# An encoder layer on one core: how far ahead expert outputs come back from DRAM, and the order of work where two stages meet

## The chip, the cores and the metric

The kernel runs on one NeuronCore of a Trainium2 chip. The metric is the device time of one execution in microseconds, lower is better. The core has five engines, each with its own in-order instruction queue: PE (matrix products), DVE (VectorE), ACT (ScalarE), POOL (GpSimd) and SP (SyncE). In this kernel SP issues nearly all plain transfers and POOL the indirect ones, which gather rows by index. All transfers are carried by 16 DMA engines. An instruction waits in its queue on semaphores, and everything behind it on that queue waits too.

## The reference, cut to what matters

One layer for 512 tokens of width 1024 in float32: layer norm, two kinds of attention, a projection and a second norm, then the part that this change is about, a mixture of 16384 single-neuron experts, and a gate and a last norm.

```python
q  = (xb @ w_q).reshape(PEER_CHUNK, PEER_HEADS, PEER_KEY_DIM)   # 8 heads
s1 = einsum('thd,kd->thk', q[..., :half], sub_keys[0])          # 128 keys
s2 = einsum('thd,kd->thk', q[..., half:], sub_keys[1])
# best 16 of each, best 16 of their sums: expert number e1 * 128 + e2
g   = softmax(cv)                        # 8 * 16 = 128 picks a token
u   = u_table[idx]                       # rows of a 16384 x 1024 table
act = g * gelu(einsum('td,ted->te', xb, u))
ffn = einsum('te,ted->td', act, v_table[idx])
h   = layer_norm(alpha * h + ffn + sigmoid(h @ W_g + b_g) * (p @ W_ple))
```

Each token picks 128 of 16384 experts. U and V, the two tables, have 64 MiB each.

## The kernel before, in words

The 512 tokens lie in four chunks of 128. They go three ways.

- **Chunk 0 by gathered rows.** For each of its 128 picks POOL fetches 128 rows of U (512 KB, tile `gat`, `GATS` = 8 buffers), and DVE multiplies them with the tokens and sums (`gather_u`, L1281). After a GELU the same is done with V rows, added into `base` (`gather_v`, L1290 and L1292). These 257 steps are spread over other work.
- **Chunks 1 to 3 densely.** The experts are 128 blocks of 128. A matrix G of gate weights (tokens by experts) is built and written to DRAM (`g_dram`). In the last long stage, the V stage, G of eight blocks is loaded at a time (`gt`, 1.5 MB, two buffers). For each block it is split into a high and a low part, V's block (512 KB, `v_raw` or `raw`) is split the same way, and PE does 18 products into six accumulators (`expert_out`).
- Dense tokens also need GELU of tokens times U. For **chunk 1** this comes from gathered U rows while routing goes on (`own_rows`), and is folded into G. For **chunks 2 and 3** (256 tokens) PE multiplies with each block of U: tile `ge`, 128 KB a block, multiplied into `gt` at L1379.

The `ge` of the first `LEAD` = 107 blocks are made early, as plain float32 products (`lead_block`, L1088), while DVE and POOL route tokens, build G and gather. Those of the first `SPILL` = 96 blocks are written to DRAM (`ge_dram`, L1072), the others are kept in SBUF. The remaining blocks get theirs inside the V stage (`expert_in`), with a split of U by ACT and DVE and 24 products.

The V stage takes the blocks in the order 96 to 127, then 0 to 95. So it first uses the kept outputs and those made along the way, and from its 33rd block on those that come back from DRAM. Block n of the stage reloads the `ge` of block n + `GE_AHEAD` (L1374, on SP). All `ge` tiles, at first writing, in `expert_in` and at reload, rotate over `GES` = 13 buffers in the order in which they are made, and a new one waits until the tile `GES` before it has been read.

What sets the order around the change: DVE and SP follow the order in which the V stage's code is written, and at the seam before it all five engines do. In block n the code asks for the G load (when due), the V load, the reload, the multiply L1379, the splits, the products, and then some gathered rows. V loads of the late blocks alternate between two sets of three buffers, `v_raw` for even n and `raw` for odd n. Until block 128 - `LEAD` the rows advance by a full share a block, later by half a share (`LATE`); all shares together are 128 - 0.5 `LEAD` - 4, which is 70.5.

The **seam** is the block of code between routing and the V stage. `BESIDE` rows of chunk 0 have been gathered before it, up to `PRE` by its end. `blocks_ahead` advances the lead blocks on PE, `cut_v` splits V's first two blocks, and `load_g` brings the first eight blocks of G on POOL's queue in two parts, of which the second part holds the tokens whose G is written last.

Of the kernel before, what the change touches and what calls it, by code (L numbers as in the profile page):

```python
# [32 lines left out]
N_U = N_D - N_S  # L33
GT = 32
GB = 8
LEAD = 107
SPILL = 96
FIRST = 8
PACE = 1.1
AHEAD = 14.0  # L40
LAG = 6.0
PRE = 42
BESIDE = 24
OWN = 1.2
OWN_G = 0.65
OWN_LATE = 10.0
# [6 lines left out]
NA_FROM = (0, 64, 192, 256)  # L53
GATS = 8
NO_GATHER = 1
GE_AHEAD = 12
GES = 13
RAWS = 4
LOW = -3.0e38
FEED_NA = 2.85  # L60
# [8 lines left out]
def tile_encoder_layer(ctx: ExitStack, tc: tile.TileContext, A: dict, out: bass.AP):  # L69
# [651 lines left out]
    for kk in range(4):  # L721
        w = stream(A["w_o"][kk * 256:(kk + 1) * 256, 0:512].rearrange("(k p) n -> p k n", p=128), [2, 512])
        for k2 in range(2):
            k = 2 * kk + k2
# [330 lines left out]
    def load_u():  # L1055
        nonlocal loaded
        if loaded < LEAD:
            if loaded % RAWS == RAWS - 1 and loaded < LEAD - 16:
                raw = rg.tile([128, 8, 128], F32, name="raw_u")
# [18 lines left out]
    def lead_block():  # L1078


        while len(raws) < (RAWS if loaded < LEAD - 16 else 3) and loaded < LEAD:
            load_u()
# [171 lines left out]
    def in_wst(n):  # L1254

        return n % 2 and 128 - LEAD < n < 124

    def load_v(n):
        raw = wst.tile([128, D], F32, name="raw", bufs=3) if in_wst(n) else pV.tile([128, D], F32, name="v_raw", bufs=3)
        nc.sync.dma_start(raw, v_rows[order[n] * 128:(order[n] + 1) * 128, :])  # L1260
        return raw
# [11 lines left out]
    def fetch_u(c, k):  # L1273
        u = pG.tile([128, D], F32, name="gat", bufs=GATS)
        nc.gpsimd.indirect_dma_start(out=u[:], out_offset=None, in_=u_rows,  # L1275
                                     in_offset=bass.IndirectOffsetOnAxis(ap=i_sel[:, c, k:k + 1], axis=0))
        return u

    def gather_u(c, k, u=None):
        u = fetch_u(c, k) if u is None else u  # L1280
        nc.vector.scalar_tensor_tensor(scr, u, 1.0, h[c], op0=OP.mult, op1=OP.mult,  # L1281
                                       accum_out=hdot[:, c, k:k + 1])
# [32 lines left out]
    def blocks_ahead(n):  # L1315
        for _ in range(8 * n):
            next(pe_work, None)
# [4 lines left out]
    with tc.manual_schedule(engines={nc.vector.engine, nc.scalar.engine, nc.tensor.engine, nc.sync.engine,  # L1322
                                     nc.gpsimd.engine}):
        gating = True
        some = [fetch_u(0, BESIDE + k) for k in range(4)]
        gt_next = load_g(0, nc.gpsimd, ((128 // GT, NTG), (0, 128 // GT)))
        some += [fetch_u(0, BESIDE + k) for k in range(4, GATS - 1)]
        blocks_ahead(2)
        v_next = [load_v(n) for n in range(2)]
        for u in range(4):  # L1330
            gather_u(0, BESIDE + u, some[u])
        blocks_ahead(2)
        v_next.append(load_v(2))
        v_cut = {}
        for n in range(2):
            v_cut[n] = cut_v(n)
            blocks_ahead(1)
        for u in range(4, 7):
            gather_u(0, BESIDE + u, some[u])
        blocks_ahead(2)  # L1340
        for k in range(BESIDE + 7, PRE):
            gather_u(0, k)
        for _ in pe_work:
            pass
    done, spent = PRE, 0
    with tc.manual_schedule(engines={nc.vector.engine, nc.sync.engine}):
        expert_in(LEAD)
        for n, i in enumerate(order):
            if n % GB == 0:
                gt = gt_next  # L1350
            if n % GB == (GB // 2 if n < 128 - LEAD + 4 else GB - 2) and n // GB < 128 // GB - 1:
                gt_next = load_g(n // GB * GB + GB)
# [37 lines left out]
            if n >= NO_GATHER:  # L1390
                spent += 1 if n + LEAD < 128 else LATE
            upto = min(len(steps), PRE + math.ceil((len(steps) - PRE) * spent / (128 - (1 - LATE) * LEAD - 3 - NO_GATHER)))
            for f in steps[done:upto]:
# [107 lines left out]
```

## Time and profile before

| | |
|---|---|
| median of 3 runs | 1694.06 us (1692.46 to 1695.3) |
| the profiled execution's own time | 1681.8 us |
| its span, first to last instruction | 1679.9 us |
| mean granted clock of PE | 0.97 |
| busy share: PE, DVE, ACT, POOL | 92%, 77%, 39%, 33% |
| moved by DMA | 462.00 MB, 275 GB/s over the span |

By stage (the view of busy time in stretches; share is the mean busy share of the 16 DMA engines, which can come out slightly above 1):

| stretch, us | what | PE busy, us | DVE busy, us | clock | DMA share | GB/s |
|---|---|---|---|---|---|---|
| 0 to 470 | norms, attention, queries | 456.35 | 344.01 | 1.00 | 0.37 | 115 |
| 470 to 893 | routing, building G, lead blocks, chunk 1's rows | 409.61 | 378.56 | 1.00 | 0.99 | 381 |
| 893 to 950 | the seam | 49.54 | 25.53 | 0.94 | 0.93 | 359 |
| 950 to 1090 | V stage, blocks with `expert_in` | 139.22 | 129.94 | 0.99 | 1.03 | 403 |
| 1090 to 1625 | V stage, blocks without | 449.83 | 379.13 | 0.93 | 0.86 | 307 |
| 1625 to 1680 | last blocks, last norm | 45.20 | 44.58 | 0.93 | 0.30 | 112 |

How to read the lines shown below. In the page's digits a span is cut into 40 slices of 42 us, a digit is the busy share in tenths. In a list by time the columns are start, duration, engine, line, operation, tiles, and in brackets the idle time before and what ended it. PE's durations overlap when products follow each other, so starts tell its pace. In a list of waits, who waited is left of the arrow, and behind the colon stand the total in us, how often, and the longest. A stretch has its bounds, length, then busy us with the count of instructions for PE, PEld (weight loads), DVE, ACT and POOL, then clock, DMA share and GB/s. A DMA queue's row has packets, MB and its share of the 16 engines' time: q1 is SP's queue, q0 POOL's.

### The profile page before, as it was taken

What the parts mean: (1) busy time and instruction counts of PE and PEld (TensorE: products, weight loads), DVE (VectorE), ACT (ScalarE), POOL (GpSimd) and SP (SyncE); (2) the same over time, 40 slices, a digit from 0 to 9 for tenths busy, and PEclk for the clock granted to TensorE, in tenths of its full rate; (3) what the DMA queues carried; (4) which work ended last, traced back from release to release, by engine and by line L of the source; (5) the groups of instructions that cost most, each with busy time, mean ns of one, the idle gap of its engine ahead of it and who ended that gap; (6) DMA issues with size and microseconds to landing.
All of it is one profiled execution on the core that took longest, in us unless ns stands there. A gap on an engine that the chain in (4) does not pass through costs nothing.

```text
span 1679.9 us, 22935 instructions
## 1 busy us (share of the span) xinstructions
PE 1549.7 (92%) x7691; PEld 1278.8 (76%) x7691; DVE 1301.7 (77%) x3019; ACT 659.5 (39%) x1235; POOL 552.8 (33%) x522
## 2 busy tenths in 40 slices
PE   8999899999999999999898899978888878888787
PEld 5788677888888888888797788866666666666666
DVE  6466784799899988988894699977677766777677
ACT  3356683433226642762353243322222222222233
POOL 1013100100143335333342555543345444445420
PEclk9999999999999999999999999999899988999999
DMA  6342330432699999999898999988788888888881
GB/s 218 84 126 75 96 107 1 141 89 65 219 340 341 401 400 410 396 415 415 287 387 340 405 406 402 399 296 306 277 310 316 314 295 292 302 312 325 295 321 76
DMA packets 195178, 462.00 MB, mean 275 GB/s; under 512 B 17778, under 2 KB 98546, under 8 KB 193524
## 3 DMA queue, kind: packets, MB, share of 16 engines
q1 hardware_dynamic: 121104, 214.07, 35.9%
q0 software_dynamic: 58400, 208.69, 33.4%
q10 hardware_dynamic: 15556, 37.76, 5.9%
q8 instruction: 61, 1.00, 0.2%
q14 instruction: 57, 0.47, 0.1%
HBM read 415.64 MB, written 41.94 MB: 272 GB/s over the span
## 4 chain that ended last, share of the span: by engine, by line
PE 38%; DMA 27%; DVE 19%; issue 10%; ACT 4%; POOL 1%; SPq 1%; ACTq 0%; DVEq 0%; POOLq 0%
DMA v_raw<-in_v_rows_dram 15%; PE mm L1088 4%; PE hp L1088 4%; PE mm L107 3%; PE tr L980 3%; PE mm L109 3%; PE pj L107 3%; PE mm L108 3%; PE pj L108 3%; DVE base L1292 3%; PE pj L109 3%; DMA raw<-in_uT_dram 3%; DMA whi<-in_u_rows_dram,s_ix 2%; DVE scr L1281 2%; DVE wlo L93 2%
## 5 line engine op out<-in xcount | busy, mean ns | idle before, releaser
L1290 POOL DMA_INDIRECT gat<-in_v_rows_dram,i_sel x128 | 208.5, 1629 | 250.1 <-DVE base L1292 213.9
L107 PE MATMUL acc<-v_hi,a_hi 128*128 128x512 f32 x450 | 185.2, 417 | 61.2 <-ACT v_hi L92 49.8
L92 ACT CAST whi<-raw 128x1024 fp32r<-128x1024 f32 (+4 forms) x117 | 117.3, 1003 | 199.3 <-DMA raw<-in_v_rows_dram 82.5
L1088 PE MATMUL mm<-whole,raw 128*128 128x256 f32 x848 | 192.0, 380 | 1.2 <-DMA raw<-in_uT_dram 1.2
L108 PE MATMUL acc<-v_lo,a_hi 128*128 128x512 f32 x450 | 183.2, 410 | 4.7 <-DVE v_lo L93 4.6
L109 PE MATMUL acc<-v_hi,a_lo 128*128 128x512 f32 x450 | 183.9, 412 | 0.0
L93 DVE TENSOR_TENSOR v_lo<-v_raw,v_hi 128x1024 fp32r<-128x1024 f32 x75 | 91.9, 1225 | 108.4 <-ACT v_hi L92 106.0
L1088 PEld LDWEIGHTS mm<-whole,raw 128*128 128x128 f32 x848 | 159.0, 191 | 21.9 <-DMA raw<-in_uT_dram 1.6
L1275 POOL DMA_INDIRECT gat<-in_u_rows_dram,i_sel x104 | 133.3, 1282 | 120.9 <-DVE scr L1281 99.2
L93 DVE TENSOR_TENSOR wlo<-raw,whi 128x1024 fp32r<-128x1024 f32 (+4 forms) x117 | 135.6, 1160 | 38.4 <-ACT whi L92 37.2
L1292 DVE SCALAR_TENSOR_TENSOR base<-gat,hdot,base 128x1024 f32<-128x1024 f32 x128 | 164.0, 1282 | 1.6
L107 PEld LDWEIGHTS acc<-v_hi,a_hi 128*128 128x128 f32 x450 | 89.0, 199 | 88.6 <-ACT v_hi L92 55.0
L92 ACT CAST v_hi<-v_raw 128x1024 fp32r<-128x1024 f32 x75 | 78.8, 1050 | 174.2 <-DMA v_raw<-in_v_rows_dram 167.5
L107 PE MATMUL acc<-whi,a_hi 128*128 128x512 f32 x306 | 123.5, 405 | 19.3 <-ACT a_hi L92 19.3
L92 ACT CAST a_hi<-gt 128x384 fp32r<-128x384 f32 x126 | 64.6, 512 | 191.8 <-DVE gt L1379 182.5
L1281 DVE SCALAR_TENSOR_TENSOR scr<-gat,h 128x1024 f32<-128x1024 f32 x104 | 127.2, 1223 | 10.7 <-DMA gat<-in_u_rows_dram,i_sel 8.7
L93 DVE TENSOR_TENSOR a_lo<-gt,a_hi 128x384 fp32r<-128x384 f32 x126 | 69.8, 554 | 72.1 <-ACT a_hi L92 72.1
L109 PE MATMUL acc<-whi,a_lo 128*128 128x512 f32 x306 | 123.7, 405 | 0.0
L1088 PE MATMUL hp<-whole,raw 128*128 128x256 f32 x512 | 117.9, 387 | 6.2 <-DMA raw<-in_uT_dram 6.2
L1032 POOL DMA_INDIRECT whi<-in_u_rows_dram,s_ix x51 | 54.3, 1064 | 208.0 <-DVE cand L883 132.1
L108 PE MATMUL acc<-wlo,a_hi 128*128 128x512 f32 x306 | 122.3, 401 | 0.0
L1088 PEld LDWEIGHTS hp<-whole,raw 128*128 128x128 f32 x512 | 98.5, 194 | 21.6 <-issue 4.5
(390 smaller groups left out, 3519.7 us busy)
## 6 DMA issues: line engine op xcount, KB each, us to landing
raw<-in_uT_dram SPq DMA_DIRECT2D x106, 512.0 KB
v_raw<-in_v_rows_dram SPq DMA_DIRECT2D x77, 512.0 KB
raw<-in_v_rows_dram SPq DMA_DIRECT2D x51, 512.0 KB
g_dram<-g_st ACTq DMA_DIRECT2D x12, 2048.0 KB
gt<-g_dram SPq DMA_DIRECT2D x15, 1536.0 KB
ge_dram<-ge ACTq DMA_DIRECT2D x96, 128.0 KB
ge<-ge_dram SPq DMA_DIRECT2D x96, 128.0 KB
raw_u<-in_uT_dram SPq DMA_DIRECT2D x22, 512.0 KB
```

The costliest lines, as they stand in the source:

```text
L92: nc.scalar.copy(hi, src)
L93: nc.vector.tensor_tensor(lo, src, r32(hi), op=OP.subtract)
L107: nc.tensor.matmul(ps, a[0], b[0], start=start, stop=False)
L108: nc.tensor.matmul(ps, a[0], b[1], start=False, stop=False)
L109: nc.tensor.matmul(ps, a[1], b[0], start=False, stop=stop)
L980: nc.tensor.matmul(ps[:, i * 128:(i + 1) * 128], oj[:, 4 * r + i, :], oi[:, 4 * r + i, :], start=True, stop=True)
L1032: nc.gpsimd.indirect_dma_start(out=u[:], out_offset=None, in_=u_rows, in_offset=bass.IndirectOffsetOnAxis(ap=ix[:, k:k + 1], axis=0))
L1088: nc.tensor.matmul(ps[:, :N_U], raw[:, k], whole[:, k, :], start=(k == 0), stop=(k == 7))
L1275: nc.gpsimd.indirect_dma_start(out=u[:], out_offset=None, in_=u_rows, in_offset=bass.IndirectOffsetOnAxis(ap=i_sel[:, c, k:k + 1], axis=0))
L1281: nc.vector.scalar_tensor_tensor(scr, u, 1.0, h[c], op0=OP.mult, op1=OP.mult, accum_out=hdot[:, c, k:k + 1])
L1290: nc.gpsimd.indirect_dma_start(out=u[:], out_offset=None, in_=v_rows, in_offset=bass.IndirectOffsetOnAxis(ap=i_sel[:, c, k:k + 1], axis=0))
L1292: nc.vector.scalar_tensor_tensor(base[c], u, hdot[:, c, k:k + 1], base[c], op0=OP.mult, op1=OP.add)
```

## The change

Six numbers change, and the code of the seam is written in another order. `LEAD` goes from 107 to 104, so three more blocks go through `expert_in`, and the shares of chunk 0's rows become 128 - 52 - 4 = 72. `GE_AHEAD` goes from 12 to 5 and `GES` from 13 to 11. `BESIDE` goes from 24 to 26 and `PRE` from 42 to 38. At the seam G's load now stands first on POOL's queue, ahead of all seven kept rows; V's first two loads come before any lead block, V's splits right behind, and the gathered rows after them.

```diff
-LEAD = 107
+LEAD = 104
-PRE = 42
-BESIDE = 24
+PRE = 38
+BESIDE = 26
-GE_AHEAD = 12
-GES = 13
+GE_AHEAD = 5
+GES = 11
...
         gating = True
-        some = [fetch_u(0, BESIDE + k) for k in range(4)]
         gt_next = load_g(0, nc.gpsimd, ((128 // GT, NTG), (0, 128 // GT)))
-        some += [fetch_u(0, BESIDE + k) for k in range(4, GATS - 1)]
+        some = [fetch_u(0, BESIDE + k) for k in range(GATS - 1)]
+        v_next = [load_v(n) for n in range(2)]
+        v_cut = {}
         blocks_ahead(2)
-        v_next = [load_v(n) for n in range(2)]
-        for u in range(4):
-            gather_u(0, BESIDE + u, some[u])
-        blocks_ahead(2)
-        v_next.append(load_v(2))
-        v_cut = {}
         for n in range(2):
             v_cut[n] = cut_v(n)
             blocks_ahead(1)
-        for u in range(4, 7):
+        v_next.append(load_v(2))
+        for u in range(GATS - 1):
             gather_u(0, BESIDE + u, some[u])
-        blocks_ahead(2)
+            if u % 3 == 2:
+                blocks_ahead(1)
         for k in range(BESIDE + 7, PRE):
             gather_u(0, k)
```

Line numbers behind the seam's code fall by three: the reload L1374 becomes L1371, the multiply L1379 becomes L1376.

SP's queue in the late V stage, with what each row waits for; before. DMAHW0 to DMAHW7 are the counters of earlier loads, used in turn; DVE and Activation are those of VectorE and ScalarE.

```order
L1374 DMA ge<-ge_dram 128x256 [waits DMAHW3_49,DVE_49]
L1260 DMA raw<-in_v_rows_dram 128x1024 [waits DMAHW4_49,Activation_49]
L1374 DMA ge<-ge_dram 128x256 [waits DMAHW5_49,DVE_49]
L1260 DMA v_raw<-in_v_rows_dram 128x1024 [waits DMAHW6_49,Activation_49]
L1374 DMA ge<-ge_dram 128x256 [waits DMAHW7_49,DVE_49]
```

And in the changed kernel.

```order
L1260 DMA v_raw<-in_v_rows_dram 128x1024 [waits DMAHW4_49,DVE_49,Activation_49]
L1371 DMA ge<-ge_dram 128x256 [waits DMAHW5_49]
L1260 DMA raw<-in_v_rows_dram 128x1024 [waits DMAHW6_49,DVE_49,Activation_49]
L1371 DMA ge<-ge_dram 128x256 [waits DMAHW7_49]
L1250 DMA gt_11139<-g_dram 128x12x256 [waits DMAHW0_49,DVE_49]
L1260 DMA v_raw<-in_v_rows_dram 128x1024 [waits DMAHW1_49,DVE_49]
```

The wait for VectorE has left the reloads and now stands on the V loads.

VectorE's queue at the seam, before: from the last one-hot matrices of G (`oh_j`) to the first splits of G (`a_lo`).

```order
L1015 TENSOR_SCALAR oh_j<-iota,eT 128x128 x8
L1281 SCALAR_TENSOR_TENSOR scr,hdot<-gat,h_77 128x1024 x4
L93 TENSOR_TENSOR v_lo<-v_raw,v_hi 128x1024 x2
L1281 SCALAR_TENSOR_TENSOR scr,hdot<-gat,h_77 128x1024 x14
L93 TENSOR_TENSOR wlo<-raw,whi 128x1024
L1379 TENSOR_TENSOR gt_8509<-gt_8509,ge 128x8x32
L93 TENSOR_TENSOR a_lo<-gt_8509,a_hi 128x384
```

And now.

```order
L1034 SCALAR_TENSOR_TENSOR wlo,hdot<-wlo,h_77 128x1024
L1015 TENSOR_SCALAR oh_j<-iota,eT 128x128 x8
L1034 SCALAR_TENSOR_TENSOR whi,hdot<-whi,h_77 128x1024
L93 TENSOR_TENSOR v_lo<-v_raw,v_hi 128x1024 x2
L1281 SCALAR_TENSOR_TENSOR scr,hdot<-gat,h_77 128x1024 x7
L93 TENSOR_TENSOR wlo<-raw,whi 128x1024
L1281 SCALAR_TENSOR_TENSOR scr,hdot<-gat,h_77 128x1024
L1376 TENSOR_TENSOR gt_8519<-gt_8519,ge 128x8x32
L1281 SCALAR_TENSOR_TENSOR scr,hdot<-gat,h_77 128x1024
L93 TENSOR_TENSOR a_lo<-gt_8519,a_hi 128x384
```

V's splits have moved ahead of the gathered rows, the multiply of the first V block stands behind 8 of those rows instead of 18, and two more rows (L1034) are done beside the building of G.

## The prediction

> **What bounds the kernel now.** I read the page first, for which stage is long and which resource is full in it.
>
> ```profile
> PE 1549.7 (92%) x7691; PEld 1278.8 (76%) x7691; DVE 1301.7 (77%) x3019; ACT 659.5 (39%) x1235; POOL 552.8 (33%) x522
> PEclk9999999999999999999999999999899988999999
> DMA  6342330432699999999898999988788888888881
> PE 38%; DMA 27%; DVE 19%; issue 10%; ACT 4%; POOL 1%; SPq 1%; ACTq 0%; DVEq 0%; POOLq 0%
> ```
>
> TensorE (PE) looks full, but its busy time is an average. The DMA digits are 9 in slices 12 to 19 and 23 to 26, and 7 or 8 in slices 27 to 39. In those late slices PEclk falls to 8 here and there. DMA holds 27% of the chain. So I cut the last third out: the chain of waits of 1120 to 1640 us, what SP's queue waits for from 1130 to 1640 us, and busy time by stage.
>
> ```profile
> by line: DMA v_raw<-in_v_rows_dram 47.7%; issue 13.2%; DVE base L1292 9.2%; DMA raw<-in_v_rows_dram 5.1%; ACT a_hi L92 4.2%; DVE gt L1379 3.2%; DVE a_lo L93 2.6%; PE acc L108 2.5%; PE acc L107 2.4%; PE acc L109 2.3%; ACT v_hi L92 2.2%; DVE
> SPq L1374 <- DVE gt L1379: 372.1, 87, 13.8
> SPq L1260 <- DVE v_lo L93: 21.6, 4, 7.2
> 1136.00:1605.00 469.00, 397.07 (x1560) 303.24 (x1559) 332.00 (x407) 132.57 (x175) 210.01 (x131) 0.92 0.85 304
> 1000.00:1080.00 80.00, 80.00 (x491) 71.74 (x490) 76.85 (x116) 32.77 (x46) 46.02 (x35) 1.00 1.03 402
> 600.00:800.00 200.00, 193.34 (x1033) 172.54 (x1032) 173.37 (x496) 90.48 (x214) 78.18 (x75) 1.00 1.02 410
> ```
>
> Nearly half of that stretch's chain is one transfer, the load of a block of V. SP spent 372.1 of these 510 us with the reload of a GELU output (L1374) at the head of its queue, waiting for VectorE's multiply of the block before (L1379). The reload sits between two V loads, so V(n+1) leaves only when block n-1 has been multiplied, two blocks before it is used. The DMA engines meanwhile have a busy share of 0.85 at 304 GB/s; in two earlier stretches they hold 1.03 and 1.02. Neither a full engine nor full DMA bounds this stage: a late request does. One period of eight blocks shows it (SP's queue, then TensorE, then the chain, then busy time in steps of 2 us: PE, PEld, DVE, ACT, POOL, clock, DMA share, GB/s).
>
> ```profile
> 1395.30 0.32 SPq L1374 DMA_DIRECT2D ge<-ge_dram  x1
> 1395.71 0.39 SPq L1250 DMA_DIRECT2D gt<-g_dram  x1
> 1396.14 2.28 SPq L1260 DMA_DIRECT2D v_raw<-in_v_rows_dram  x1
> ...
> 1404.05 1.05 SPq L1260 DMA_DIRECT2D v_raw<-in_v_rows_dram  x1
> 1418.08 0.32 SPq L1374 DMA_DIRECT2D ge<-ge_dram  x1
> ...
> 1400.16 0.39 PE L109 MATMUL acc<-v_hi,a_lo 128*128 128x512 f32 x1
> 1401.52 0.39 PE L109 MATMUL acc<-v_hi,a_lo 128*128 128x512 f32 x1
> 1413.53 0.79 PE L107 MATMUL acc<-v_hi,a_hi 128*128 128x512 f32 x1 [7.42 <-ACT v_hi L92]
> ...
> 1396.14 16.27 DMA v_raw<-in_v_rows_dram
> ...
> 1406.00:1408.00 2.00, 0.11 (x1) 0.00 (x0) 0.00 (x0) 0.00 (x0) 0.00 (x0) 1.00 1.03 399
> 1408.00:1410.00 2.00, 0.00 (x0) 0.00 (x0) 0.00 (x0) 0.00 (x0) 0.00 (x0) 0.57 1.03 398
> 1414.00:1416.00 2.00, 1.53 (x4) 0.94 (x4) 2.00 (x3) 1.38 (x2) 0.00 (x0) 0.50 0.09 37
> 1416.00:1418.00 2.00, 2.00 (x7) 1.51 (x6) 1.96 (x4) 0.70 (x1) 1.33 (x1) 0.50 0.00 0
> ```
>
> The 1.5 MB of gates (gt) go out at 1395.71 and the V block right behind them lands 16.27 us after its own issue. TensorE waits 7.42 us for it and then runs at clock 0.50. VectorE's stall has held SP and POOL back too, so once the backlog has landed DMA falls to 0.09 and then 0.00. Every period loses time twice: compute waits for DMA, then DMA for compute.
>
> **The change part by part.** Two rates first, as counts of the multiply L1379, one per block, up to the 21st block and from it on.
>
> ```profile
> L1379 DVE TENSOR_TENSOR gt<-gt,ge x21: 418/420/422, 950.6 to 1090.4; 128x256 f32<-128x256 f32 x21
> L1379 DVE TENSOR_TENSOR gt<-gt,ge x99: 415/419/425, 1090.4 to 1624.1; 128x256 f32<-128x256 f32 x99
> DMA packets 60840, 142.74 MB, mean 304 GB/s; under 512 B 5035, under 2 KB 33048, under 8 KB 60816
> q0 software_dynamic: 4953, 18.00, 56.9%
> q1 hardware_dynamic: 5907, 14.10, 45.9%
> ```
>
> Early blocks, which also make one expert block's activations: 139.8 us / 20 = 6.99 us each. Late blocks: 533.7 / 98 = 5.45 us.
>
> *Reloads 5 ahead, 11 buffers.* The buffer that a reload fills was last read by block n+12-13 = n-1. Now it is block n+5-11 = n-6. Each V load waits by itself for the split of six blocks back, so the reload adds no later wait: the order's rows show VectorE's counter gone from L1371 and now on the V loads. SP can run up to six blocks ahead instead of two, and the gates with it. At 4.7 us a block (below) that is 28 us of lead against the 16.27 us that the worst landing took; the stall should go.
>
> What then holds a late block? The 469 us window has 88 blocks (11 gate loads of eight), 5.33 us each.
> - DMA: share 0.85 x 5.33 / 1.03 = 4.40 us when saturated.
> - TensorE: six matmuls start in 1401.52 - 1400.16 = 1.36 us, so eighteen take 4.08 us at full clock.
> - VectorE: 332.00 / 88 = 3.77 us; ScalarE 132.57 / 88 = 1.51 us.
>
> The floor is 4.40 us, the ceiling the 5.45 of now. I take 4.70 us: it is 0.85 x 5.33 / 0.97, a share between the present 0.85 and the 1.02 to 1.03 of the stretches whose requests were always waiting, and nearer to those, because one or two gathered rows per block still make the engines take turns. (The Trainium skill, "DMA: Bandwidth & Descriptors", Specifications, puts HBM's limit for one core at about 358 GB/s. By it, 142.74 MB / 88 = 1.62 MB per block would need an estimated 4.5 us, not 4.40. The rows of 402 GB/s over 80 us and 410 over 200 us lie above that limit, so the measurement decides and I keep 4.40.)
>
> *Lead 104.* Three blocks become early ones. Measured to the same block, before: 20 x 6.99 + 98 x 5.45 = 673.5 us. After: 23 x 6.99 + 95 x 4.70 = 607.3 us. **Sum: -66 us.** At 4.40 it would be -95, at 5.45 +5 us.
>
> *The seam.* Behind the last gate products VectorE, POOL and DMA look like this (POOL's gathers and gate loads, a row of VectorE, the stretch up to the first V block, and the first product of V).
>
> ```profile
> 879.58 0.95 POOL L1275 DMA_INDIRECT gat<-in_u_rows_dram,i_sel  x1 [0.30 <-issue]
> 900.02 0.97 POOL L1250 DMA_DIRECT2D gt<-g_dram  x1 [19.50 <-PE tr L980]
> 910.03 0.78 POOL L1250 DMA_DIRECT2D gt<-g_dram  x1 [9.04 <-DMA g_dram<-g_st]
> 911.12 1.01 POOL L1275 DMA_INDIRECT gat<-in_u_rows_dram,i_sel  x1 [0.31 <-issue]
> ...
> 918.72 1.28 DVE L93 TENSOR_TENSOR v_lo<-v_raw,v_hi 128x1024 fp32r<-128x1024 f32 x1 [20.09 <-ACT v_hi L92]
> ...
> 955.01 0.40 PE L107 MATMUL acc<-v_hi,a_hi 128*128 128x512 f32 x1
> ...
> 910.00:950.00 40.00, 35.34 (x146) 29.49 (x146) 20.09 (x31) 5.89 (x11) 24.99 (x22) 0.92 1.03 406
> 895.00:900.00 5.00, 5.00 (x39) 4.77 (x38) 3.56 (x6) 2.25 (x4) 0.00 (x0) 1.00 0.13 45
> ```
>
> From 910 on DMA is at 1.03, so bytes set the end. Nine transfers of 512 KB leave this stretch: three lead blocks (107 to 104) and six gathers (42 - 24 = 18 becomes 38 - 26 = 12). At 0.524 MB / 406 GB/s = 1.29 us each that is -11.6 us. Two of the gathers go to the stage before, saturated too: +2.6 us. The other four join the V blocks; their number per block stays at about 3 early and 1.5 late (257 - 38 steps over 72 shares, 257 - 42 over 70.5 before), so the rates above contain them. Against it: POOL now has the gate loads first, and their second half left only at 910.03, when the G products had been written. The four gathers issued by 879.58 now queue behind that and leave after 911. I put this at +2 us: DMA was full at their old place too, but five microseconds at 895 stand at 0.13. Queued behind the gate wait on POOL are all seven kept rows; VectorE waits for them, but it idled 20.09 us before 918.72 anyway, until the first V split. **Seam: -7 us**, between -15 (the first multiply now stands behind 8 gathers instead of 18 in VectorE's order) and +6 (all four gathers and the gap at 895 lost).
>
> *Fewer buffers while the lead blocks are made:* the spilled outputs rotate over 11 instead of 13, and a new one waits for the write to DRAM of the one 11 before.
>
> ```profile
> ACT ge L1070 <- DMA ge_dram<-ge: 9.2, 3, 3.1
> ```
>
> With 13 that held ScalarE in three places. ScalarE is busy 39% of the span, so I take 0, with 0 to +5 us as ends. The three exchanged blocks' splits lie inside the 6.99 us.
>
> Total -66 - 7 = -73 us against the profiled execution's own 1681.8: 1609 us. The median of the runs shown is 1694.06, 0.7% above that execution, so I scale: 1609 x 1694.06 / 1681.8 = **1620 us**.
>
> **The rivals.**
>
> *A. Half the stall stays (chance 0.16).* SP runs ahead, but gates and V still share one queue, and a load occupies one of eight DMA counters used in turn (the DMAHW numbers in the order's rows), so at most about four blocks are in flight, not six. Then a block costs 5.1 us: 23 x 6.99 + 95 x 5.1 = 645.3, -28; with -3 at the seam 1681.8 - 31 = 1651, scaled 1663. For it: 1.5 MB at half of 402 GB/s take 7.8 us, almost two blocks. Against: four blocks at 4.7 are 19 us, still over 16.27.
>
> *B. The wait was never the cause (0.06).* If V blocks were late only because the engines are full of other bytes, late blocks stay at 5.45: +5 us, with -7 at the seam -2, 1692 us scaled, no change. Against it stand the 0.09 and 0.00 behind the stall: requests were missing.
>
> *C. Gathers starve: slower (0.04).* SP's deeper queue takes the engines from POOL's rows. A late block gathers 1.52 x 0.524 = 0.80 MB. POOL's queue must move that in less than 5.45 us, 146 GB/s or 36% of 402; below that share VectorE, which does multiplies and gathered rows in one order, holds everything. At 33% a block takes 6.0 us: 23 x 6.99 + 95 x 6.0 = 730.8, +57; 1732 after the seam, 1745 scaled. Against it: between 1000 and 1080, with V and u loads steadily on SP's queue, POOL's queue (q0) had 56.9 against 45.9. (The Trainium skill, "DMA: Bandwidth & Descriptors", Queues, rings and completion order, says that a DMA engine takes its queues in turn, a packet at a time. By that rule q0 keeps half, an estimated 0.80 MB / 201 GB/s = 4.0 us a block, and C falls away; the trace's 56.9 to 45.9 agrees.)
>
> *D. Saturation is reached (0.14).* A late block at 4.45 and the seam at -12: 23 x 6.99 + 95 x 4.45 = 583.5, -90 - 12; 1580, scaled 1591.
>
> **How the numbers follow.** Forecast 0.60 (a late block of 4.55 to 4.95, 1606 to 1644 us), A 0.16, D 0.14, B 0.06, C 0.04. The range takes the forecast, most of A and the upper half of D: 1592 to 1664 us. A measurement of this kernel separates about 0.2% from no change. Faster by more than that: forecast, A, D and part of B, 0.92; within it: 0.04, from B; slower: 0.04, C.
>
> **What would show it.** SP's waits of L1371 for the multiply should fall from 372 us to nearly nothing, and its queue should now wait for VectorE's splits at the V loads (L1260). V should lose its 47.7% of the late chain; the DMA share of the late window should rise from 0.85 to about 0.97, the clock from 0.92 to almost 1. Gate loads should lie 8 x 4.7 = 38 us apart instead of 42.6. The first product of V should start about 7 us earlier. I am wrong on the mechanism if the L1371 wait goes and landings of V behind the gates still leave 7 us gaps on TensorE (A), or if VectorE waits for gathered rows (C); wrong on the seam if the first product is no earlier than 955.

## The result, and the profile after

| | before | after |
|---|---|---|
| median, same chip | 1694.47 us (4 executions) | 1565.53 us (1562.71 to 1568.51, 4 executions) |
| profiled execution; its span | 1681.8; 1679.9 us | 1564.57; 1562.7 us |
| mean granted clock of PE | 0.97 | 0.988 |

The ratio is 0.9241, interval [0.9221, 0.9261]: faster by 129 us. The forecast was 1620 us with a range of 1592 to 1664, so the direction was right and the size too small. Ratios are of fast executions alone: one of the four of the run that leaves out 6 of 18 products took 4012.79 us and is not in its ratio.

The page of the changed kernel (busy time, the digits of the clock and of DMA over 40 slices of 39 us, the chain):

```profile
PE 1510.1 (97%) x7715; PEld 1268.2 (81%) x7715; DVE 1302.4 (83%) x3022; ACT 660.3 (42%) x1238; POOL 558.7 (36%) x522
PEclk9999999999999999999999998999999999999999
DMA  6333231143369999999989999999999999999982
PE 69%; DMA 13%; DVE 11%; issue 4%; ACT 2%; POOL 1%; SPq 1%; another core or an unknown queue 0%; ACTq 0%; DVEq 0%; POOLq 0%
```

The 7s and 8s of the late DMA slices are gone, and so are the dips of the clock there. PE now holds 69% of the chain instead of 38%. The late stage of the changed kernel follows: its chain of waits, what SP's queue waited for (us, times, longest), and busy time beside an earlier, saturated stretch.

```profile
by line: PE acc L107 29.7%; PE acc L108 29.6%; PE acc L109 29.5%; DMA v_raw<-in_v_rows_dram 11.7%; issue 0.5%; ACT a_hi L92 0.3%; ACT v_hi L92 0.0%; ACTq L92 0.0%
```

```profile
SPq L1371 <- DMA gt<-g_dram: 47.9, 12, 5.7
SPq L1260 <- DVE v_lo L93: 46.7, 13, 8.6
SPq L1260 <- DVE wlo L93: 39.7, 20, 3.6
```

```profile
1120.00:1505.00 385.00, 381.50 (x1647) 309.73 (x1647) 351.99 (x435) 136.46 (x184) 227.20 (x139) 1.00 1.04 395
1000.00:1080.00 80.00, 80.00 (x480) 71.24 (x479) 78.38 (x118) 33.43 (x47) 46.95 (x36) 1.00 1.03 398
```

The reload's wait for the multiply, 372.1 us before, is not in that list at all; SP now waits mostly at the V loads, for VectorE (`v_lo` and `wlo` are V's splits). V fell from 47.7% of the late chain to 11.7%. PE is busy for 381.50 of 385 us at clock 1.00, and DMA is as full as in the earlier stretch.

Where the time went is read from the starts of the multiply, one per block, up to the 24th and from it to the 119th; before, then after.

```profile
L1379 DVE TENSOR_TENSOR gt<-gt,ge x24: 418/420/422, 950.6 to 1108.8; 128x256 f32<-128x256 f32 x24
L1379 DVE TENSOR_TENSOR gt<-gt,ge x96: 415/419/425, 1108.8 to 1624.1; 128x256 f32<-128x256 f32 x96
```

```profile
L1376 DVE TENSOR_TENSOR gt<-gt,ge x24: 418/419/422, 936.0 to 1107.7; 128x256 f32<-128x256 f32 x24
L1376 DVE TENSOR_TENSOR gt<-gt,ge x96: 416/419/431, 1107.7 to 1505.0; 128x256 f32<-128x256 f32 x96
```

The first multiply came 14.6 us earlier, but of that only 1.1 us is left at the 24th, less than such a start scatters (see "The lead and the seam"). The next 95 blocks took 397.3 us instead of 515.3, 4.18 instead of 5.42 us each: -118.0 us. The rest, from the 119th multiply to the end of the span, grew from 55.8 to 57.7 us. Sum: -1.1 - 118.0 + 1.9 = -117.2, the difference of the spans. Practically the whole gain lies in the late blocks.

### The profile page after: what moved, and what is told of

Its sections match the earlier page's. It is cut to its first block, busy times and chain, and to the rows that moved or that the text cites. A ratio compares the mean times of both kernels' runs of the same rounds, so it can differ in the third digit from the quotient of the medians.

```text
span 1562.7 us, 22922 instructions
## 1 busy us (share of the span) xinstructions
PE 1510.1 (97%) x7715; PEld 1268.2 (81%) x7715; DVE 1302.4 (83%) x3022; ACT 660.3 (42%) x1238; POOL 558.7 (36%) x522
## 4 chain that ended last, share of the span: by engine, by line
PE 69%; DMA 13%; DVE 11%; issue 4%; ACT 2%; POOL 1%; SPq 1%; another core or an unknown queue 0%; ACTq 0%; DVEq 0%; POOLq 0%
PE acc L107 9%; PE acc L108 9%; PE acc L109 9%; PE mm L1088 5%; PE hp L1088 5%; DMA raw<-in_uT_dram 4%; PE mm L107 3%; PE pj L107 3%; PE mm L109 3%; PE tr L980 3%; PE mm L108 3%; PE pj L109 3%; PE pj L108 3%; DMA v_raw<-in_v_rows_dram 3%; DMA wlo<-in_u_rows_dram,s_ix 2%
## 5 line engine op out<-in xcount | busy, mean ns | idle before, releaser
L1290 POOL DMA_INDIRECT gat<-in_v_rows_dram,i_sel x128 | 213.6, 1668 | 140.5 <-DVE base L1292 116.0
L1088 PE MATMUL mm<-whole,raw 128*128 128x256 f32 x864 | 196.2, 381 | 0.0
L107 PE MATMUL acc<-v_hi,a_hi 128*128 128x512 f32 x456 | 180.1, 396 | 7.5 <-ACT a_hi L92 7.5
L1088 PEld LDWEIGHTS mm<-whole,raw 128*128 128x128 f32 x864 | 162.7, 192 | 21.0
L109 PE MATMUL acc<-v_hi,a_lo 128*128 128x512 f32 x456 | 179.7, 395 | 0.0
L108 PE MATMUL acc<-v_lo,a_hi 128*128 128x512 f32 x456 | 179.4, 394 | 0.0
L107 PE MATMUL acc<-whi,a_hi 128*128 128x512 f32 x300 | 119.2, 397 | 3.5 <-ACT a_hi L92 3.5
L109 PE MATMUL acc<-whi,a_lo 128*128 128x512 f32 x300 | 119.3, 398 | 0.0
L1015 DVE TENSOR_SCALAR oh_j<-iota,eT 128x128 f32<-128x128 f32 x384 | 109.8, 360 | 0.0
L1088 PE MATMUL hp<-whole,raw 128*128 128x256 f32 x448 | 102.4, 384 | 5.4 <-DMA raw<-in_uT_dram 5.4
```

Of the source, the lines that this page charges most:

```text
L107: nc.tensor.matmul(ps, a[0], b[0], start=start, stop=False)
L108: nc.tensor.matmul(ps, a[0], b[1], start=False, stop=False)
L109: nc.tensor.matmul(ps, a[1], b[0], start=False, stop=stop)
L1015: nc.vector.tensor_scalar(oj[:, i], iota, eT[:, 1, t0 + i:t0 + i + 1], eT[:, 2, t0 + i:t0 + i + 1], op0=OP.is_equal, op1=OP.mult)
L1088: nc.tensor.matmul(ps[:, :N_U], raw[:, k], whole[:, k, :], start=(k == 0), stop=(k == 7))
```

## The experiments

All ratios are to the kernel before, run on the same chip beside each group; its medians there were 1692.15, 1693.22, 1689.51 and 1686.22 us. "A late block" is the time between the 24th and the 119th multiply over 95, unless another count stands there. A reload of block n "waits on n-1" when its buffer was last read by the multiply of that block. (The change sets five constants, not six.)

### Which part of the change: the reload alone, and all but the reload

The kernel before with the reload 5 ahead and 13 buffers (waits on n-8):

```diff
-GE_AHEAD = 12
+GE_AHEAD = 5
```

> The kernel before with only the reload distance changed: 5 blocks ahead instead of 12, still 13 buffers, lead 107, old seam. The buffer that a reload fills was then last read 8 blocks earlier. Theory R (the reload's wait alone held the late V stage): the 21st block starts at 1090 us as before, then 98 blocks at the 4.18 us of the changed kernel (397.3 us for 95 blocks) give 410 us and the tail 57 us: about 1557 us of span, 1555 to 1572 us of time. Rival S (lead 104 and the new seam are needed for the gain, since the runs before them fill the same DMA engines): at least 1600 us.

Measured: 1568.11 us, ratio 0.9266 [0.9238, 0.9293]. The multiplies of that kernel:

```profile
L1379 DVE TENSOR_TENSOR gt<-gt,ge x24: 417/419/421, 950.3 to 1113.6; 128x256 f32<-128x256 f32 x24
L1379 DVE TENSOR_TENSOR gt<-gt,ge x96: 414/417/421, 1113.6 to 1507.5; 128x256 f32<-128x256 f32 x96
```

And the changed kernel with the reload put back so that it waits on n-1 (10 ahead, 11 buffers):

```diff
-GE_AHEAD = 5
+GE_AHEAD = 10
```

> The changed kernel with the reload 10 blocks ahead in its 11 buffers, so that the buffer was again last read by the block before: everything changed but the wait. Theory R: the 24th block starts at 1108 us as in the changed kernel, then 95 blocks at the old 5.45 us and the tail: about 1680 us of span, 1675 to 1700 us, no change against the kernel before. Rival S: at most 1660 us.

Measured: 1698.76 us, ratio 1.0032 [1.0001, 1.0062]; a late block 5.50 us. SP's longest wait of its late stage:

```profile
SPq L1371 <- DVE gt L1376: 394.5, 90, 14.1
```

The wait of 372 us is back under its new line number, and the gain is gone with it. The reload distance alone gives the gain to within the intervals, at (1507.5 - 1113.6) / 95 = 4.15 us a late block; lead, seam and buffers without it give none. What else this one edit moved is the second suspect, below.

### The lead and the seam

The changed kernel with `LEAD` as before and 13 buffers, then with three early blocks more:

```diff
-LEAD = 104
+LEAD = 107
```

> The changed kernel with its new seam, its BESIDE and PRE and its reload 5 ahead, but LEAD 107 and 13 buffers as before. The reload alone (old seam, LEAD 107, 13 buffers) took 1568, the changed kernel 1565.5. If LEAD 104 gives back what the seam gains (three more early blocks): 1558 to 1563, faster than the changed kernel. If LEAD is neutral now that TensorE holds both stages: 1563 to 1568. If fewer early blocks crowd the gathers: above 1570.

```diff
-LEAD = 104
+LEAD = 101
```

> The changed kernel with LEAD 101 in place of 104. With the new seam and the near reload, LEAD 107 took 1569.4 and 104 took 1565.5, so three more early blocks were worth -4 us. If that goes on: 1559 to 1563, faster than the changed kernel. If the DMA engines set the whole stretch from 470 us on, their bytes being the same: 1563 to 1568. If the early blocks, slower each by 3 us, cost more than the seam saves: above 1569.

Measured: 1569.43 us, ratio 0.9272 [0.9229, 0.9316], with 107; 1575.84 us, 0.9336 [0.9299, 0.9373], with 101. The first does not stand apart from the changed kernel, the second is slower by about 1%. First to 24th multiply with 107, then with 101:

```profile
L1376 DVE TENSOR_TENSOR gt<-gt,ge x24: 418/419/422, 948.4 to 1113.6; 128x256 f32<-128x256 f32 x24
```

```profile
L1376 DVE TENSOR_TENSOR gt<-gt,ge x24: 417/419/422, 935.8 to 1118.1; 128x256 f32<-128x256 f32 x24
```

With the new seam and the old lead the V stage begins at 948.4, with the old seam (the reload alone, above) at 950.3: the new order of the seam seems worth 2 us there, but that is not resolved. In the changed kernel and the four that differ from it only in `GE_AHEAD` (7, 8, 9 and 10), the instructions up to the first multiply stand in the same order, and it starts anywhere from 936.0 to 942.9 us, the 24th from 1107.7 to 1114.1. What lies outside this scatter is the earlier start with `LEAD` 104, 5.5 to 12.4 us ahead of 948.4, and that the early blocks give it back: (1107.7 - 936.0) / 23 = 7.47 us each, 7.37 to 7.50 in those five kernels, against (1113.6 - 948.4) / 23 = 7.18 with 107 (where the last three of the 23 are already late ones).

A reason can be counted. When the 24th multiply starts, all 128 blocks of U have been read in either case (107 or 104 of them before the stage), the same blocks of V and G, and 106 or 105 rows of chunk 0 gathered (42 + 21 shares of 3.05, or 38 + 22 of 3.04). All of that crosses DMA engines that are nearly full at the seam, at a share of 0.96 and 0.93, and full behind it, at 1.02 and 1.01 (the changed kernel, then the reload alone):

```profile
893.00:950.00 57.00, 47.24 (x223) 40.02 (x222) 25.88 (x43) 12.88 (x22) 23.75 (x22) 0.91 0.96 369
950.00:1110.00 160.00, 156.16 (x930) 139.06 (x930) 146.59 (x220) 63.16 (x88) 87.33 (x67) 0.98 1.02 393
```

```profile
893.00:950.00 57.00, 47.85 (x226) 40.86 (x224) 25.75 (x41) 9.38 (x18) 27.09 (x23) 0.97 0.93 359
950.00:1110.00 160.00, 153.84 (x899) 136.15 (x899) 140.73 (x213) 62.01 (x89) 84.40 (x65) 0.98 1.01 391
```

By this count, bytes taken out of the seam come due a few blocks later, at nearly the same rate.

### A second suspect: ScalarE's order

The scheduler that places ScalarE's casts moved them when the reload distance changed. In the kernel before, and in the one with all but the reload, they come in uneven groups; in the changed kernel and with the reload alone they alternate strictly. ScalarE of the kernel before, in the period that the prediction shows:

```profile
1402.97 0.51 ACT L92 CAST a_hi<-gt 128x384 fp32r<-128x384 f32 x1 [2.63 <-DVE gt L1379]
1412.43 1.04 ACT L92 CAST v_hi<-v_raw 128x1024 fp32r<-128x1024 f32 x1 [8.95 <-DMA v_raw<-in_v_rows_dram]
1413.98 1.05 ACT L92 CAST whi<-raw 128x1024 fp32r<-128x1024 f32 x1 [0.51 <-DMA raw<-in_v_rows_dram]
1415.65 1.05 ACT L92 CAST v_hi<-v_raw 128x1024 fp32r<-128x1024 f32 x1 [0.62 <-DMA v_raw<-in_v_rows_dram]
1418.16 0.51 ACT L92 CAST a_hi<-gt 128x384 fp32r<-128x384 f32 x1 [1.47 <-DVE gt L1379]
```

The cast of `a_hi` at 1418.16 stands behind three casts of V, the last of them for a later block, each of which waits for its load. (The last thing that it waited for was the multiply, so this period alone shows no loss by the order.) So the order could have been part of the cause. First the kernel before, with the loop cut in two at block 24 and ScalarE in the written order (V of block n, then a of block n) behind that:

```diff
-    with tc.manual_schedule(engines={nc.vector.engine, nc.sync.engine}):
-        ... for n, i in enumerate(order):
+    with tc.manual_schedule(engines={nc.vector.engine, nc.sync.engine}):
+        ... for n in range(24):
+    with tc.manual_schedule(engines={nc.vector.engine, nc.sync.engine, nc.scalar.engine}):
+        for n in range(24, 128):
```

> The kernel before, unchanged in its reload distance of 12, its lead and its seam; only ScalarE's casts follow the written order (cast of V's block, cast of a, next block) from block 24 on, where the scheduler had put them in uneven groups (two or three a_hi, then two casts of V). The changed kernel, the reload alone and the kernel without gathered V rows all had the even order, the two slow kernels the uneven one, so this order is a second suspect. Theory S (SP's wait at the reload is the cause, the order only follows the scheduler's guess): the late block stays at 5.4 to 5.5 us and the time within 10 us of 1692. Theory O (the order is the cause): the late block falls to about 4.2 us and the time to 1565 to 1590. Both partly: 4.6 to 5.1 us a block, 1610 to 1660.

Measured: 1665.44 us, ratio 0.983 [0.9776, 0.9885]; a late block 5.09 us, between the two theories and nearer to SP's wait. Then the reverse, the changed kernel with the uneven order of the kernel before written out for ScalarE:

```diff
+    seq = "V24 A24 V25 V26 A25 A26 V27 V28 A27 A28 V29 A29 A30 V30 ..."
...
+        while ("V", n) not in tiles or ("A", n) not in tiles:
+            cast(*seq.pop(0))
```

> The changed kernel, with ScalarE's casts of blocks 24 to 123 put into the uneven order that they have in the kernel before (V25 V26 A25 A26 V27 V28 A27 ..., A for the cast of a); SP's, VectorE's, POOL's and TensorE's rows are the changed kernel's. Fourth corner of a square: reload waits on n-1 with the uneven order 1693, with an even order 1665; on n-6 with an even order 1566. If the two causes add up, the uneven order costs its 28 us again: 1585 to 1600, 4.4 to 4.5 us a block. If the order only hurts where V comes late (a cast of V that waits for its load holds up the cast of a behind it): 1563 to 1572, and the whole gain is that of the reload. With 12 products the uneven order was 41 us slower than the even one (1609 against 1568), which speaks for a cost: above 1600 is possible too.

Measured: 1574.55 us, ratio 0.9335 [0.9309, 0.9361], between the two expected ranges; a late block 4.28 us, and 4.17 from the 41st multiply on. In 1200 to 1400 us of that kernel:

```profile
1200.00:1400.00 200.00, 200.00 (x871) 163.05 (x870) 184.93 (x219) 70.86 (x96) 121.46 (x75) 1.00 1.04 396
```

| ratio to before | uneven order | even order |
|---|---|---|
| reload waits on n-1 | 1 | 0.983 |
| reload waits on n-6 | 0.9335 | 0.9241 |

So the order is a second, small cause: 28 us where V comes late (19 to 38 by the interval), and about 16 where it does not (0.0094 of 1686). Of those 16, about 6 us stand ahead of block 24 in the profile (its 24th multiply started at 1113.9, in the changed kernel at 1107.7), where ScalarE's order is not forced; that is within the scatter of this start. Both runs also cut the loop, and no run cuts it without forcing an order, so what the cut itself costs is not shown. In the 200 us shown PE has no gap in spite of the uneven order (in the changed kernel it is busy for 197.90 of them). Freeing SP's queue carries 112 of 128 us (1 - 0.9335 against 1 - 0.9241, of 1686) without any help from the order.

### How much run-ahead is needed

The changed kernel with its 11 buffers and the reload 9, 8 and 7 ahead, which waits on n-2, n-3 and n-4. With 9 ahead the scheduler still put a few of ScalarE's casts in uneven groups, so there is a second kernel with 9 ahead and ScalarE in its written order.

```diff
-GE_AHEAD = 5
+GE_AHEAD = 9
```

> The changed kernel with the reload 9 blocks ahead and its 11 buffers, so that the reload of block n waits for the multiply of block n-2 in place of n-6: SP may run two blocks ahead of VectorE, where before it was one. If each block of run-ahead counts until the V buffers (3 and 3) are the limit: 4.5 to 4.8 us a block, 1595 to 1630. If one more block is enough, because the chain load, cast, product then fits between two multiplies: 4.17 to 4.25 us, 1565 to 1575. If the wait on one block or two is the same to the chain: above 5.3 us, 1680 to 1695.

> The changed kernel with the reload 9 ahead (its wait is on the multiply of block n-2) and ScalarE in written order from block 24 on, so that the order is that of the kernel before with ScalarE's written order, which waited on n-1 and took 5.08 us a block, 1665. Without the written order, 9 ahead took 5.06 us and 1654.5. If one more block of run-ahead is worth nothing: 5.0 to 5.1 us, 1645 to 1660. If the order of ScalarE hid its worth: 4.6 to 4.8 us, 1610 to 1630.

> The changed kernel with the reload 8 ahead: the wait is on the multiply of block n-3, ScalarE has the changed kernel's even order. Theory: a V load must leave so early that the gates' 1.5 MB and the blocks ahead of it in the queue have landed; those landings took 12.7 to 20.8 us, 3 to 5 blocks of 4.15 us. V then leaves 4 blocks ahead. If run-ahead counts up to 16 us: 4.4 to 4.7 us a block, 1590 to 1620. If 3 blocks are enough: 4.15 to 4.25 us, 1565 to 1572. If the worth comes only at n-6: above 1640.

> The changed kernel with the reload 7 ahead: the wait is on the multiply of block n-4, V leaves 5 blocks ahead, 20 us at 4.15 us a block, as long as the longest median landing (20.8 us for the gates). If run-ahead counts up to that landing: 4.15 to 4.3 us a block, 1565 to 1580. If only n-6 gives the whole: 4.4 us, 1590 and above.

| waits on | ScalarE's order | us | ratio | late block, us |
|---|---|---|---|---|
| n-1 (before) | uneven | | 1 | 5.42 |
| n-1 (before) | written | 1665.44 | 0.983 [0.9776, 0.9885] | 5.09 |
| n-2 | partly uneven | 1654.53 | 0.9775 [0.9734, 0.9816] | 5.07 |
| n-2 | written | 1636.79 | 0.9684 [0.9632, 0.9736] | 4.90 |
| n-3 | alternating | 1622.68 | 0.9601 [0.9557, 0.9645] | 4.74 |
| n-4 | alternating | 1572.14 | 0.931 [0.9265, 0.9356] | 4.24 |
| n-6 (after) | alternating | 1565.53 | 0.9241 [0.9221, 0.9261] | 4.18 |

Busy time in the same 200 us with the wait on n-2 (written order), n-3 and n-4:

```profile
1200.00:1400.00 200.00, 177.58 (x711) 140.12 (x710) 152.47 (x181) 59.20 (x80) 100.20 (x61) 0.92 0.91 330
```

```profile
1200.00:1400.00 200.00, 185.62 (x770) 148.64 (x769) 163.91 (x194) 62.32 (x85) 111.70 (x65) 0.96 0.96 348
```

```profile
1200.00:1400.00 200.00, 197.68 (x848) 159.57 (x847) 180.28 (x215) 70.98 (x95) 124.40 (x72) 0.99 1.03 389
```

The wait on n-4 came out as expected, the one on n-3 a little above its expected range, and n-2 in written order between its two theories. Each block of run-ahead is worth something, and the largest step, 0.50 us a block, lies between n-3 and n-4. With n-4 V leaves five blocks ahead, 5 x 4.24 = 21 us, with n-3 four, 4 x 4.74 = 19 us. Both would cover the landing of 16.27 us quoted in the prediction, but that is not the longest: in the chains of 1150 to 1500 us, V behind the gates took up to 18.97 us with n-3 and up to 17.65 us with n-4. The longest with n-3 and what follows it, then the longest with n-4:

```profile
1352.62 18.97 DMA v_raw<-in_v_rows_dram
1361.17 0.52 ACT L92 CAST a_hi<-gt 128x384 fp32r<-128x384 f32 x1 [2.87 <-PE acc L109]
1371.67 1.04 ACT L92 CAST v_hi<-v_raw 128x1024 fp32r<-128x1024 f32 x1 [9.98 <-DMA v_raw<-in_v_rows_dram]
1372.62 0.51 ACT L92 CAST a_hi<-gt 128x384 fp32r<-128x384 f32 x1
1373.18 0.60 PE L107 MATMUL acc<-whi,a_hi 128*128 128x512 f32 x1 [3.82 <-ACT a_hi L92]
```

```profile
1391.00 17.65 DMA v_raw<-in_v_rows_dram
```

PE multiplies with `whi`, so the cast of `a_hi` at 1372.62 belongs to the block before the one whose V has just been cast: in the alternating order V of the next block stands ahead of a, and V is wanted a block early. That leaves three blocks, 14 us, for a landing of up to 18.97 us with n-3, and four, 17 us, for up to 17.65 us with n-4. From 1150 to 1450 us PE stood 19.9 us for `a_hi` with n-3 and 2.5 us with n-4. The place of the step agrees with the landings behind the gates; no run changes these landings by themselves, and none has n-3 or n-4 in written order, so the steps of the table are not clean where the order changes. With n-4 SP's queue still stood 134.1 us of the 300 us from 1150 to 1450 at the reload:

```profile
SPq L1371 <- DVE gt L1376: 134.1, 54, 4.4
```

That wait costs little any more, 4.24 against 4.18 us a block. Not the time at the head of a queue decides, but how far ahead of use the load behind it leaves.

### What holds a late block at 4.18 us now

PE and the DMA engines both look full, and either could be the bound. First 12 of the 18 products from block 24 on (the product of a's low part is left out, and with it that part of the output):

```diff
-            mm3(acc[c][hf], (ah[:, cs], al[:, cs]), (vh[:, hs], vl[:, hs]), n == 0, n == 127)
+            if n < 24:
+                mm3(acc[c][hf], (ah[:, cs], al[:, cs]), (vh[:, hs], vl[:, hs]), n == 0, n == 127)
+            else:
+                nc.tensor.matmul(acc[c][hf], ah[:, cs], vh[:, hs], start=False, stop=False)
+                nc.tensor.matmul(acc[c][hf], ah[:, cs], vl[:, hs], start=False, stop=(n == 127))
```

> The changed kernel with 12 of the 18 products per block of V from the 25th block on (the low part of the gates times the high part of V is left out of the sum); all loads, splits and gathered rows stay. Theory P (PE's 18 products, 4.08 us, hold the late block of 4.18 us, and DMA has room): the block falls to about 4.0 us, 1.64 MB at 405 to 410 GB/s, and the time by 15 us or more, to 1550 us or less. Rival Q (the DMA engines hold it, at 395 GB/s and a share of 1.04): block and time stay, 1560 to 1568 us, and PE gets idle time in front of each block.

Measured: 1609.04 us, ratio 0.9502 [0.9459, 0.9546], slower than with all 18. The result says nothing on the bound, for the scheduler had moved ScalarE's casts into uneven groups again, and PE waited for them (1200 to 1500 us):

```profile
PE acc L1310 <- ACT a_hi L92: 97.7, 49, 8.2
```

The same with the loop cut at block 24 and ScalarE in written order behind it:

> The changed kernel with 12 of the 18 products of expert_out from block 24 on (the products of a's low half with V's high half are left out, so the output lacks them) and ScalarE in the written order from there on, so that only PE's load differs. TensorE then needs about 12 x 0.23 = 2.7 us a block, VectorE still about 3.8 us (352 of 385 us at 4.17 us a block), the DMA engines what they need. Theory P (the 18 products alone hold the late block, the transfers have room): the block falls to VectorE's 3.8 to 3.95 us, the time to 1535 to 1550. Theory Q (the transfers are as full as PE at 395 GB/s and hold the block just below it): 4.05 to 4.18 us a block, 1553 to 1566. If the granted clock falls with the gaps on TensorE and 12 products become late themselves: above 1570.

Then, with all 18 products, the gathered V rows left out (chunk 0 lacks its expert sum):

```diff
-                yield lambda c=c, k=k: gather_v(c, k)
+                yield lambda: None
```

> The changed kernel without the 128 gathered rows of V and their multiply-adds (the experts' sum for the first 128 tokens is left out); gathered rows of U stay. Where no rows are left, from about the 39th block on, a block moves 0.85 MB instead of 1.64 and VectorE has 2.2 us of work. Theories P and Q both expect the block at PE's own pace there, 4.08 to 4.12 us, with the DMA share near 0.55; the time falls by 5 to 10 us. If the block stays at 4.18 us, PE's own pace in this stage is that, and DMA holds nothing.

And both together:

> The changed kernel with both of the things left out that alone moved nothing: 12 of the 18 products from block 24 on (a's low half times V's high half is missing) and the gathered V rows (the first 128 tokens lack their expert sum), ScalarE in written order. If TensorE (18 products, 4.1 us) and the DMA engines (1.65 MB a block at 396 GB/s, 4.15 us) are two limits of nearly equal height, then taking both away must move what neither alone did: the block falls to TensorE's 12 products, 2.7 to 3.1 us, and the time by 95 x 1.1 to 1.4 us, to 1430 to 1465. If a third thing (the landing of V or gates, a chain through the casts, SP's queue) holds 4.1 us: 1550 to 1566 again.

| left out | us | ratio | block, 41st to 119th multiply |
|---|---|---|---|
| nothing (after) | 1565.53 | 0.9241 | 4.16 us |
| 6 of 18 products | 1568.29 | 0.9255 [0.9206, 0.9304] | 4.12 us |
| gathered V rows | 1566.13 | 0.9249 [0.9216, 0.9283] | 4.14 us |
| both | 1454.98 | 0.8604 [0.8563, 0.8645] | 2.76 us |

Busy time without six products, without the rows, and without both:

```profile
1200.00:1500.00 300.00, 233.25 (x872) 168.33 (x871) 275.73 (x328) 106.96 (x145) 182.26 (x110) 0.94 1.04 396
```

```profile
1200.00:1500.00 300.00, 300.00 (x1305) 244.63 (x1304) 147.05 (x219) 107.12 (x146) 0.00 (x0) 1.00 0.64 207
```

```profile
1200.00:1400.00 200.00, 200.00 (x871) 162.99 (x870) 153.72 (x217) 105.82 (x145) 0.00 (x0) 1.00 0.92 311
```

Relieving PE leaves DMA at 1.04 and 396 GB/s; relieving DMA (0.64) leaves PE without a gap. Neither moves the time (without the rows, 5 to 10 us less had been expected), both together take 1.4 us off a block. The late stage stands under two limits of nearly the same height, PE's 18 products at 4.14 us and a second one at 4.12. That is theory Q, and PE's pace is what the prediction had put at 4.08. Leaving out the rows takes work from VectorE and POOL too, so these runs alone do not say that the second limit is the transfers. Two readings speak for it: 396 GB/s is what the changed kernel moved, and without six products the chain of 1200 to 1500 us is loads of V for 58%, against about 28% VectorE, which was busy for 275.73 of the 300 us.

## Why the prediction was wrong in size

**The wait and its effect: right.** The 372.1 us at the reload were the cause, as forecast; the reload alone gives the gain and putting it back takes the gain away. V's share of the late chain, the move of SP's waits to the splits (46.7 and 39.7 us) and the clock (0.92 to 1.00) came as listed. The prediction did not price the clock's part. (The Trainium skill, "TensorE: Matmul & The Clock Gate", HAM oscillation — how this bites in real kernels, says that gaps on PE above about 3.4 us lower its clock. The traces agree: 0.50 behind the gap of 7.42 us before, and 1.00 now, where the longest wait on PE between 1150 and 1450 us is 2.1 us.)

**The late block: the step that failed.** "DMA: share 0.85 x 5.33 / 1.03 = 4.40 us when saturated", and on top of it the choice of 4.70 us, "0.85 x 5.33 / 0.97". It measured 4.18. The first formula treats busy share as an amount of work that stays the same when a block gets shorter. It is not, as the late rows of SP's queue (q1) and POOL's (q0) show: packets, MB, share of the 16 engines' time; before over 469 us, then after over 385 us, with its total.

```profile
q1 hardware_dynamic: 41989, 73.90, 44.9%
q0 software_dynamic: 18827, 68.55, 40.3%
```

```profile
DMA packets 64779, 151.96 MB, mean 395 GB/s; under 512 B 5326, under 2 KB 35200, under 8 KB 64755
q1 hardware_dynamic: 44616, 78.35, 55.1%
q0 software_dynamic: 20139, 73.32, 48.6%
```

A packet of q1 held an engine for 0.449 x 469 x 16 / 41989 = 80 ns before and 76 ns after, one of q0 for 161 and 149 ns. The same bytes took less busy time once the stage no longer stalled; why, no run shows. The 5.33 us are off too: the 469 us hold 88 loads of V, but 86 multiplies, so a block took 5.45 us there, as the prediction's own rate says. With 5.45 the formula gives 4.50, still further off, so part of its error had cancelled by luck. By bytes the floor would have come out near: 142.74 MB / 86 blocks = 1.66 MB, at the 402 GB/s that the prediction had shown 4.13 us; the changed kernel moved 151.96 MB in 92 blocks, 1.65 MB each, and at its 395 GB/s that is the 4.18 measured. The prediction worked out bytes per block (1.62 MB, by 88), but only to answer the rule of 358 GB/s. (The Trainium skill, "Perfetto Trace Analysis", Identifying the Most-Contended Engine, says to judge DMA by the bandwidth it reaches and not by occupancy, which it calls misleading. The rows above agree. I had not weighed that rule.)

The second choice, a share of 0.97 because the stage would stay short of saturation, describes a kernel that exists: with the wait on n-3 the share was 0.96 and a late block took 4.74 us. With n-6 the stage goes on to 1.04, with the same one or two gathered rows a block (139 of POOL's gathers in the 92 blocks) that were to keep it below. The loads of G, forecast 38 us apart, took 100.63 us for three periods, 33.5 us each:

```profile
1278.84 0.39 SPq L1250 DMA_DIRECT2D gt<-g_dram  x1
...
1379.47 0.37 SPq L1250 DMA_DIRECT2D gt<-g_dram  x1
```

With 4.18 in place of 4.70, 95 x 0.52 = 49 us more would have been forecast (28 of them from 0.97 in place of 1.03, 21 from the share taken as work), which is the miss to within 5 us: 1609 forecast for the profiled execution, 1564.57 measured. The other 10 of the 54 us between the two medians come from the scaling by 1694.06 / 1681.8; the changed kernel's median lies only 0.06% above its profiled execution.

**The rivals.** D had the right state, saturation, but at 4.45 us, by the same formula. A (5.1 us) is what a wait on n-1 in written order or on n-2 gives (5.09; 5.07 and 4.90), not n-6: SP did stand 118.4 of the 385 us waiting for its own earlier loads, 47.9 of them shown above at the reloads, but PE lost nothing by it. B falls by the run with the reload alone (4.15 us). C falls: q0 keeps 48.6 against 55.1 of q1, and VectorE's 351.99 of 385 us still fit.

**Lead and seam: wrong as parts; the sum is too small to judge.** To the 24th multiply the prediction's numbers give -7 at the seam and 23 x 6.99 against 20 x 6.99 + 3 x 5.45 = +4.6, together -2.4 us; -1.1 was measured, but the 24th multiply scatters by 6.4 us over the five kernels named above, so this is no confirmation. The first product of V came at 941.51, not 7 but 13.5 us earlier than 955.01 (9.1 to 14.8 us earlier in those five), and the early blocks took 7.47 us in place of 6.99:

```profile
941.51 0.79 PE L107 MATMUL acc<-v_hi,a_hi 128*128 128x512 f32 x1 [3.69 <-ACT a_hi L92]
```

The seam's count took nine transfers out and charged two of them to the stage before; that the early rate of 6.99 contains the others was the slip, as far as the count of bytes above goes. Where DMA is full, what is put off comes due again.

**Fewer buffers: right.** ScalarE's wait for spilled outputs with 11 buffers is what it was with 13:

```profile
ACT ge L1070 <- DMA ge_dram<-ge: 9.2, 3, 3.1
```

**Not foreseen:** that changing a distance on SP's queue makes the scheduler reorder ScalarE. It helped here, by about 16 us of the 129, and spoilt the first run with 12 products.

## What to carry to other kernels

A refill into a rotating buffer waits for that buffer's last reader, and in an in-order queue it makes every load behind it wait as well; compare the distance at which each load leaves with the depth that its own buffers would allow, and give the refill at least that much slack. When a stall goes, price the stage that is left by bytes over the best bandwidth seen and by instructions over their pace, and not by scaling a busy share that was measured with the stall in place. Before reading one change as one cause, look whether the scheduler has moved another engine's order along with it.

## What was not expected of the hardware

The busy share of the DMA engines is not proportional to what they move. In 200 us of the late stage, with the wait on n-2, n-3 and n-4, they had 0.91 at 330 GB/s, 0.96 at 348 and 1.03 at 389: from the first to the last of these the share grows by 13% and the bytes by 18%. Here a share of 0.91 in a stage that stalls hid more room than the missing tenth: 330 to 395 GB/s is 20%. And 395 GB/s held for 385 us with gathered rows and plain loads mixed, while PE ran at full clock.
